# Mixture of experts on one core: TensorE's order fixed step by step, each pair's gates beside the preceding pair's down projection, and a group's gather in one piece

## The chip, the core and the metric

One core of a Trainium2 chip runs the whole program. Its engines each work through a queue of their own: TensorE (PE; its weight loads are listed apart as PEld), VectorE (DVE), ScalarE (ACT), GpSimd (POOL) and SyncE (SP), whose queue issues the transfers of weights. The metric is the device time of one execution in microseconds (us).

## The reference

An encoder of two layers on 256 tokens of width 1024. Layer 0 mixes tokens by multi-head latent attention, layer 1 by Hyena long convolutions. Each mixer is followed by a mixture of experts: 16 experts in four groups of four, of which a token takes the best group and in it the best two experts.

```
def hier_moe(h, wg, bg, we, be, w_gate, w_up, w_down):
    ...
    combine = jnp.sum(jax.nn.one_hot(expert, N_EXPERTS, dtype=jnp.float32) * weights[..., None], axis=1)
    combine = combine.astype(t.dtype)
    out = jnp.zeros_like(t)
    for e in range(N_EXPERTS):
        a = jax.nn.silu(t @ w_gate[e]) * (t @ w_up[e])
        out = out + combine[:, e:e + 1] * (a @ w_down[e])
    return out.reshape(B, S, D)
...
        x = x + g2[:, None, :] * hier_moe(h, moe_wg[i], moe_bg[i], moe_we[i], moe_be[i],
                                          moe_w_gate[i], moe_w_up[i], moe_w_down[i])
```

A gate and an up matrix are 1024 x 256 each, a down matrix 256 x 1024.

## The kernel before

The change lies in the function of the experts, `moe(l, ss)` (layer `l` is 0 or 1). Each expert has 64 slots for tokens. Tokens are brought into the slots, and results back to the tokens, by matmuls with one-hot matrices. Two experts are worked on at once, a pair, each in 64 columns of TensorE, so there are eight pairs, two to a group. The pieces, and the names that the trace has for them:

- `hot(g)`: VectorE makes the one-hots `OH` of group g (L1176). Those of the groups after the first wait for the last evacuation of the gather before (`evac`).
- `gather(g, h)`: half of the gathering matmuls of a group, 16 of 128x256 into two banks `xt_ps` (L1310). Each bank is emptied into `XT` in two halves, the first by ScalarE (L1317), the second by VectorE (L1319).
- `gate_up(pair)`: 16 matmuls into `gu_ps` (L1399; in the trace each f32 matmul is two records, so 32). Then, for the first pair of a group, `group_out`: four matmuls `oht_ps` (L1338) that turn the one-hots over, VectorE's copy to `OHT` (L1339) and the combining weights `ws` (L1343). Then ScalarE's silu `sg` (L1407) and VectorE's product `aa` (L1409), which takes `sg`, `ws` and `gu_ps`.
- `down(pair, aa)`: two transposes `at_ps` (L1417), VectorE's copy `aT` (L1419), eight matmuls `dn_ps` (L1426, 16 records), and for each of its two halves VectorE's `yg` (L1429), ScalarE's `yH` (L1431) and VectorE's rest `yL` (L1433).
- `scatter(pair, ys)`: eight matmuls `acc` (L1445) that add `yH` and `yL` to the four accumulators.

The loop over ten steps writes gate_up(step), after odd steps the gather of the next group, scatter(step - 2) and down(step - 1). That is the order in which the program is written, not the one in which it runs: a scheduler that simulates a timeline decides the order on every engine, and it also puts other work between: in layer 0 that of the Hyena filters (matmuls `fh`, `fn`, `fi`, `fg`, `ff`, with VectorE's work on `fab` and others) and `ada_ps` (L398), the conditioning of the next layer. Only for pair 0 is TensorE's order written out by hand, by `ordered()`. What stands inside keeps its order on TensorE, and each such block comes behind the end of the one before, the instruction in `tail[0]`:

```
    @contextmanager
    def ordered():
        with ExitStack() as z:
            if tail[0] is not None:
                z.enter_context(tc.issue_after(tail[0]))
            z.enter_context(tc.manual_schedule(engines={mybir.EngineType.PE}))
            yield
        tail[0] = next(i for i in reversed(nc.cur_bb.bb.instructions) if i.engine == mybir.EngineType.PE)
```

After step 0 stands a branch (`tc.If`, L1463) that all engines pass: behind it lies the case of an expert with more tokens than slots, which this input doesn't take. PSUM banks: two for `dn_ps`, `oht_ps`, `at_ps` and `xt_ps` together, one for `gu_ps`, four for `acc`. Weights come in pieces of 1 MB through a class `Stream`, which issues the next transfer when a piece has been used up (`st.done`). After the experts of layer 0 the accumulators are copied to `x` and squared (`scr`) for the next norm; after those of layer 1 they are copied (L1472) and sent out.

Of the kernel before, what the change touches and what calls it, by code (L numbers as in the profile page):

```python
# [11 lines left out]
F32 = mybir.dt.float32  # L12
# [7 lines left out]
P = 128  # L20
# [6 lines left out]
CAP = 64  # L27
# [143 lines left out]
def trunk(ctx, tc, A, out):  # L171
    nc = tc.nc
# [261 lines left out]
    tail = [None]  # L434
# [79 lines left out]
    q = psF("rb_ps")  # L514
# [647 lines left out]
    def moe(l, ss):  # L1162
        with ExitStack() as es:
# [134 lines left out]

            def gather(g, h):
                XTs, OH = prep[g]  # L1300
                XT = gp.tile([P, 4, 256], F32, name="XT", tag="XT", bufs=3 + l)
                XTs.append(XT)
                for k2 in (2 * h, 2 * h + 1):
                    q = psA("xt_ps")
                    for kk in range(2):
                        k = 2 * k2 + kk
                        i = 0
                        for src in (xH, xL):
                            for t in range(2):
                                nc.tensor.matmul(q[:, kk * 256:(kk + 1) * 256], src[:, t, k * P:(k + 1) * P], OH[:, t, :],  # L1310
                                                 start=(i == 0), stop=(i == 3))
                                i += 1
                    for kk in range(2):
                        k = 2 * k2 + kk
                        qv = q[:, kk * 256:(kk + 1) * 256]
                        if kk == 0:
                            eva = nc.scalar.activation(XT[:, k % 4, :], qv, AF.Identity, scale=a[:, k:k + 1], bias=b[:, k:k + 1])  # L1317
                        else:
                            evac[0] = nc.vector.tensor_scalar(XT[:, k % 4, :], qv, a[:, k:k + 1], b[:, k:k + 1], op0=ALU.mult, op1=ALU.add)  # L1319
                if g == 0 and h == 1:  # L1320

                    with tc.issue_after(eva.ins):
                        nc.scalar.activation(sm.tile([P, 1], F32, name="warm"), C("ones", 0, 1), AF.Silu)

            def group(g):
                hot(g)
                for h in range(2):
                    gather(g, h)


            def group_out(g, OH):
# [52 lines left out]
            with tc.tile_pool(name="moew", bufs=2) as wp:  # L1384
                def gate_up(pair):
                    g, p2 = divmod(pair, 2)
                    XT, OH = prep[g]
                    es2 = (2 * pair, 2 * pair + 1)
                    q = psG("gu_ps")
                    for h in range(2):  # L1390
                        if pair == 0:
                            with ordered():
                                gather(0, h)
                        GU = [st.get("gu", l, e, h).rearrange("p (k n) -> p k n", k=4) for e in es2]
                        with ordered() if pair == 0 else nullcontext():
                            for k in range(4 * h, 4 * h + 4):
                                for i in range(2):
                                    c0 = (2 * p2 + i) * CAP
                                    nc.tensor.matmul(q[i * 64:(i + 1) * 64, :], XT[h][:, k % 4, c0:c0 + CAP], GU[i][:, k % 4, :],  # L1399
                                                     start=(k == 0), stop=(k == 7))  # L1400
                        for e in es2:
                            st.done("gu", l, e, h)
                    if p2 == 0:
                        outs[g] = group_out(g, OH)
                    ws = outs[g][1]
                    sg = wp.tile([P, 256], F32, name="sg", tag="sg", bufs=l + 1)
                    nc.scalar.activation(sg, q[:, :256], AF.Silu)  # L1407
                    aa = wp.tile([P, 256], F32, name="aa", tag="aa", bufs=l + 1)
                    nc.vector.scalar_tensor_tensor(out=aa, in0=sg, scalar=ws[:, p2:p2 + 1], in1=q[:, 256:], op0=ALU.mult, op1=ALU.mult)  # L1409
                    return aa  # L1410

                def down(pair, aa):
                    g, p2 = divmod(pair, 2)
                    es2 = (2 * pair, 2 * pair + 1)
                    q = psA("at_ps")
                    for j in range(2):
                        nc.tensor.transpose(q[:, j * P:(j + 1) * P], aa[:, j * P:(j + 1) * P], ident)  # L1417
                    aT = wp.tile([P, 2, P], F32, name="aT", tag="aT", bufs=l + 1)
                    nc.vector.tensor_copy(aT, q[:, :256].rearrange("p (a b) -> p a b", a=2))  # L1419
                    DN = [st.get("dn", l, e).rearrange("p (k n) -> p k n", k=2) for e in es2]  # L1420
                    ys = []
                    for n in range(2):
                        q = psA("dn_ps")
                        for j in range(2):
                            for i in range(2):
                                nc.tensor.matmul(q[i * 64:(i + 1) * 64, :], aT[:, j, i * 64:(i + 1) * 64], DN[i][:, j, n * 512:(n + 1) * 512],  # L1426
                                                 start=(j == 0), stop=(j == 1))
                        yg = wp.tile([P, 512], F32, name="yg", tag="yg", bufs=l + 1)
                        nc.vector.tensor_tensor(yg, q, grow[1][:, n * 512:(n + 1) * 512], op=ALU.mult)  # L1429
                        yH = wp.tile([P, 512], F32R, name="yH", tag="yH")  # L1430
                        nc.scalar.copy(yH, yg)  # L1431
                        yL = wp.tile([P, 512], F32R, name="yL", tag="yL")
                        nc.vector.tensor_tensor(out=yL, in0=yg, in1=yH.bitcast(F32), op=ALU.subtract)  # L1433
                        ys.append((yH, yL))
                    for e in es2:
                        st.done("dn", l, e)
                    return ys

                def scatter(pair, ys):
                    g, p2 = divmod(pair, 2)  # L1440
# [8 lines left out]
                aas, yss, outs = {}, {}, {}  # L1449
                for step in range(10):  # L1450
                    if step == 7 and l == 0:
                        st.hold = 4
                    if step < 8:
                        aas[step] = gate_up(step)
                        if step % 2 == 1 and step < 7:
                            group(step // 2 + 1)
                    if 0 <= step - 2:
                        scatter(step - 2, yss.pop(step - 2))
                    if step == 0:

                        top = nc.values_load(most.bitcast(I32)[0:1, 0:1], min_val=0, max_val=2 ** 31 - 1)
                        fp = wp.tile([P, 512], F32, name="fb", tag="yg", bufs=l + 1)
                        with tc.If(top > int(np.float32(CAP).view(np.int32)), label=f"beyond{l}"):  # L1463
                            beyond(fp)
                    if 0 <= step - 1 < 8:
                        yss[step - 1] = down(step - 1, aas.pop(step - 1))
                ss = None if l else sm.tile([P, 2, 2], F32, name="ss", tag="ss")
                for t in range(2):
                    for n in range(2):
                        sl = slice(n * 512, (n + 1) * 512)  # L1470
                        if l:
                            (nc.scalar.copy if n else nc.vector.tensor_copy)(x[:, t, sl], acc[t, n])  # L1472
                            nc.sync.dma_start(out[:, t, sl], x[:, t, sl])
                        else:
                            scr = wp.tile([P, 512], F32, name="scr", tag="yg", bufs=1)
# [102 lines left out]
```

## Time and profile before

| | |
|---|---|
| device time, three runs | 675.87 us median, 675.6 to 677.37 |
| the profiled execution | 673.48 us, of which the profile's span is 671.7 |
| mean granted clock of TensorE | 0.968 of full speed |
| TensorE busy | 612.9 us, 91% of the span |
| VectorE, ScalarE busy | 387.3 us (58%), 235.1 us (35%) |
| DMA | 183.02 MB, mean 272 GB/s |

The profile was taken from one execution, whose time lies a little under the median of the three runs. All times in it count from the start of the span.

### The profile page before, as it was taken

Reading aid. Unit: us, or ns where it says so; the run is one execution under the profiler, and the core shown is the slowest. Engines: PE = TensorE matmul, PEld = TensorE weight load, DVE = VectorE, ACT = ScalarE, POOL = GpSimd, SP = SyncE. Lnnn points to the kernel's source line nnn. Section 1 sums busy time; section 2 is a strip of 40 time slices with the busy share of each in tenths; the row PEclk is TensorE's granted clock in tenths of the full one; section 3 lists DMA queues with packets and bytes.
Section 4 is the critical chain, followed back from the end, with each engine's and each line's share of the span. In section 5 each row is a group of like instructions: output and inputs, shape, how many; then the busy total and the mean of one; then the engine's idle time right before and its main releaser. Section 6 shows DMA issues by size and latency. Waiting matters only on the chain. (4 is left out here: it accounts for less than half of the span.)

```text
span 671.7 us, 8605 instructions
## 1 busy us (share of the span) xinstructions
PE 612.9 (91%) x3149; PEld 359.1 (53%) x3149; DVE 387.3 (58%) x894; ACT 235.1 (35%) x475; POOL 6.1 (1%) x61
## 2 busy tenths in 40 slices
PE   5988888999879789999997999999998899999996
PEld 2656444656655435335435979458766434444432
DVE  7648797895585453442476386478785723333333
ACT  4626553574244212201155644324413312111111
POOL 0000000000000000000000000000000000000000
PEclk9897979999988999999997999999999799999999
DMA  8963999452943789697996656880069278999701
GB/s 333 418 278 119 412 422 419 195 188 91 370 198 134 300 350 381 255 357 306 399 412 240 245 194 237 348 356 1 0 257 387 108 252 363 421 393 407 293 1 62
DMA packets 26818, 183.02 MB, mean 272 GB/s; under 512 B 3089, under 2 KB 3474, under 8 KB 5522
## 3 DMA queue, kind: packets, MB, share of 16 engines
q1 hardware_dynamic: 26192, 180.84, 68.1%
q10 hardware_dynamic: 578, 1.57, 0.6%
q8 instruction: 26, 0.43, 0.3%
q14 instruction: 22, 0.18, 0.1%
HBM read 181.35 MB, written 1.05 MB: 272 GB/s over the span
## 5 line engine op out<-in xcount | busy, mean ns | idle before, releaser
L1399 PE MATMUL gu_ps<-wt,XT 128*64 128x512 f32 x448 | 112.1, 599 | 8.1 <-DVE aa L1409 4.1
L1399 PEld LDWEIGHTS gu_ps<-wt,XT 128*64 128x64 f32 x448 | 33.8, 137 | 65.3 <-issue 54.7
L1429 DVE TENSOR_TENSOR yg<-dn_ps,g1row 128x512 f32<-128x512 f32 x32 | 22.0, 688 | 81.0 <-PE dn_ps L1426 80.0
L1426 PE MATMUL dn_ps<-wt,aT 128*64 128x512 f32 x224 | 57.5, 597 | 0.0
L1431 ACT CAST yH<-yg 128x512 fp32r<-128x512 f32 x32 | 19.8, 617 | 105.4 <-DVE yg L1429 105.4
L1068 PE MATMUL psu<-hT,wt 128*128 128x256 f32 x192 | 44.2, 381 | 0.0
L678 DVE TENSOR_TENSOR wt<-wt 128x512 fp32r<-128x512 f32 x66 | 41.8, 684 | 2.9 <-ACT wt L677 2.2
L1068 PEld LDWEIGHTS psu<-hT,wt 128*128 128x128 f32 x192 | 35.9, 191 | 9.4 <-issue 2.4
L677 ACT CAST wt<-wt 128x512 fp32r<-128x512 f32 x66 | 36.1, 619 | 13.7 <-PE psu L690 6.1
L1319 DVE TENSOR_SCALAR XT<-xt_ps,modA,modT 128x256 f32<-128x256 f32 x32 | 17.4, 543 | 40.4 <-ACT XT L1317 40.0
L398 PE MATMUL ada_ps<-wt,csil 128*32 128x512 f32 x264 | 38.7, 628 | 0.0
L1068 PE MATMUL psu<-zH,wt 128*128 128x256 f32 x192 | 38.3, 293 | 0.0
L1317 ACT ACTIVATE XT<-xt_ps,modT,modA 128x256 f32<-128x256 f32 x32 | 18.0, 564 | 50.1 <-PE xt_ps L1310 50.0
L1426 PEld LDWEIGHTS dn_ps<-wt,aT 128*64 128x64 f32 x224 | 17.3, 136 | 30.6 <-issue 29.1
L1068 PEld LDWEIGHTS psu<-zH,wt 128*128 128x128 f32 x192 | 30.3, 189 | 2.4 <-ACT up L1073 0.8
L1433 DVE TENSOR_TENSOR yL<-yg,yH 128x512 fp32r<-128x512 f32 x32 | 22.1, 690 | 14.5 <-ACT yH L1431 14.4
L1310 PE MATMUL xt_ps<-OH,xH 128*128 128x256 f32 x128 | 28.8, 307 | 0.7 <-DVE m L1268 0.6
L1310 PE MATMUL xt_ps<-OH,xL 128*128 128x256 f32 x128 | 27.4, 292 | 0.6 <-DVE xL L1262 0.5
L1310 PEld LDWEIGHTS xt_ps<-OH,xH 128*128 128x128 f32 x128 | 21.3, 197 | 11.4 <-issue 4.1
L1068 PE MATMUL psu<-zL,wt 128*128 128x256 f32 x96 | 27.0, 281 | 0.0
L1076 DVE SCALAR_TENSOR_TENSOR uc<-up,vec,uc 128x256 f32<-128x256 f32 x24 | 11.6, 483 | 26.1 <-ACT uc L1075 26.1
L690 PE MATMUL y_ps<-wt 128*128 128x512 f32 x96 | 24.6, 403 | 0.0
(357 smaller groups left out, 1094.1 us busy)
## 6 DMA issues: line engine op xcount, KB each, us to landing
wt<-in_gu SPq DMA_DIRECT2D x56, 1024.0 KB, 7.7
wt<-in_adas SPq DMA_DIRECT2D x40, 1024.0 KB, 10.5
wt<-in_dn SPq DMA_DIRECT2D x28, 1024.0 KB, 6.9
wt<-in_win SPq DMA_DIRECT2D x12, 1024.0 KB, 7.7
wt<-in_ada SPq DMA_DIRECT2D x8, 1024.0 KB, 17.7
wx<-in_gu SPq DMA_DIRECT2D x8, 1024.0 KB, 7.6
wt<-in_wo SPq DMA_DIRECT2D x4, 1024.0 KB, 5.7
wt<-in_wout SPq DMA_DIRECT2D x4, 1024.0 KB, 10.9
```

Of the source, the lines that this page charges most:

```text
L398: nc.tensor.matmul(q[g * 32:(g + 1) * 32, :], w.to_broadcast([P, 32]), W[:, g * 512:(g + 1) * 512], start=first, stop=(k == 7))
L677: nc.scalar.copy(Hi[:, sl], W[:, sl])
L678: nc.vector.tensor_tensor(Lo[:, sl], W[:, sl], Hi[:, sl].bitcast(F32), op=ALU.subtract)
L690: nc.tensor.matmul(yq[t, n], z[:, k, cols(t)], W[:, kk, n * 512:(n + 1) * 512], start=(k == 0 and f == 1), stop=(k == 7 and l == 1))
L1068: nc.tensor.matmul(q[:, :S], w[:, k, mm * P:(mm + 1) * P], h[:, k, :], start=(k == 0 and w is terms[0][0] and h is terms[0][1]), stop=(k = ...
L1310: nc.tensor.matmul(q[:, kk * 256:(kk + 1) * 256], src[:, t, k * P:(k + 1) * P], OH[:, t, :], start=(i == 0), stop=(i == 3))
L1317: eva = nc.scalar.activation(XT[:, k % 4, :], qv, AF.Identity, scale=a[:, k:k + 1], bias=b[:, k:k + 1])
L1399: nc.tensor.matmul(q[i * 64:(i + 1) * 64, :], XT[h][:, k % 4, c0:c0 + CAP], GU[i][:, k % 4, :], start=(k == 0), stop=(k == 7))
L1426: nc.tensor.matmul(q[i * 64:(i + 1) * 64, :], aT[:, j, i * 64:(i + 1) * 64], DN[i][:, j, n * 512:(n + 1) * 512], start=(j == 0), stop=(j = ...
L1429: nc.vector.tensor_tensor(yg, q, grow[1][:, n * 512:(n + 1) * 512], op=ALU.mult)
L1431: nc.scalar.copy(yH, yg)
L1433: nc.vector.tensor_tensor(out=yL, in0=yg, in1=yH.bitcast(F32), op=ALU.subtract)
```

## The change

Every step of the loop is now one block under `ordered()`: on TensorE gate_up(s), down(s - 1), scatter(s - 2), then what was the second half of gate_up and the first of down, as `gated(s)` (group_out in even steps, `sg`, `aa`, transposes, `aT`), and in odd steps the one-hots and both halves of the next group's gather. So `down` gets `aT` where it got `aa`. `tail[0]` is cleared before the loop and behind the branch. Numbers of buffers change: XT 2 in layer 0 and 4 in layer 1 (from 3 and 4), and sg, aa, yg, fb and scr the pool's two in both layers (from 1 in layer 0 and 2 in layer 1).

```diff
@@ -1298,7 +1298,7 @@
-                XT = gp.tile([P, 4, 256], F32, name="XT", tag="XT", bufs=3 + l)
+                XT = gp.tile([P, 4, 256], F32, name="XT", tag="XT", bufs=2 + 2 * l)
@@ -1321,11 +1321,6 @@
-            def group(g):
-                hot(g)
-                for h in range(2):
-                    gather(g, h)
@@ -1384,39 +1379,41 @@
                     for h in range(2):
                         if pair == 0:
-                            with ordered():
-                                gather(0, h)
+                            gather(0, h)
...
+                    return q
+
+
+                def gated(pair, q):
+                    g, p2 = divmod(pair, 2)
                     if p2 == 0:
-                        outs[g] = group_out(g, OH)
+                        outs[g] = group_out(g, prep[g][1])
                     ws = outs[g][1]
...
-                    return aa
-
-                def down(pair, aa):
-                    g, p2 = divmod(pair, 2)
-                    es2 = (2 * pair, 2 * pair + 1)
                     q = psA("at_ps")
                     for j in range(2):
                         nc.tensor.transpose(q[:, j * P:(j + 1) * P], aa[:, j * P:(j + 1) * P], ident)
                     aT = wp.tile([P, 2, P], F32, name="aT", tag="aT", bufs=l + 1)
                     nc.vector.tensor_copy(aT, q[:, :256].rearrange("p (a b) -> p a b", a=2))
+                    return aT
+
+                def down(pair, aT):
+                    es2 = (2 * pair, 2 * pair + 1)
@@ -1446,24 +1443,32 @@
                 for step in range(10):
                     if step == 7 and l == 0:
                         st.hold = 4
-                    if step < 8:
-                        aas[step] = gate_up(step)
+                    with ordered():
+                        q = gate_up(step) if step < 8 else None
+                        if 0 <= step - 1 < 8:
+                            yss[step - 1] = down(step - 1, aTs.pop(step - 1))
+                        if 0 <= step - 2:
+                            scatter(step - 2, yss.pop(step - 2))
+                        if step < 8:
+                            aTs[step] = gated(step, q)
                         if step % 2 == 1 and step < 7:
-                            group(step // 2 + 1)
-                    if 0 <= step - 2:
-                        scatter(step - 2, yss.pop(step - 2))
+                            g = step // 2 + 1
+                            hot(g)
+                            for h in range(2):
+                                gather(g, h)
                     if step == 0:
...
+                        tail[0] = None
-                    if 0 <= step - 1 < 8:
-                        yss[step - 1] = down(step - 1, aas.pop(step - 1))
```

What this moves, at three places, the first on two engines. In layer 1, on TensorE, from the down projection of pair 0 to the gather of group 2, before:

```order
L1426 MATMUL dn_ps<-wt,aT 64x512 x8
L1338 MATMUL oht_ps<-tok,OH 128x160 x2
L1445 MATMUL acc<-yH,OHT 128x512 x2
L1445 MATMUL acc<-yL,OHT 128x512 x2
L1338 MATMUL oht_ps<-tok,OH 128x160 x2
L1417 MATMUL at_ps<-cst,aa 128x128 x2
L1445 MATMUL acc<-yH,OHT 128x512 x2
L1399 MATMUL gu_ps<-wt,XT 64x512 x13
L1445 MATMUL acc<-yL,OHT 128x512 x2
L1426 MATMUL dn_ps<-wt,aT 64x512 x8
L1399 MATMUL gu_ps<-wt,XT 64x512 x3
L1310 MATMUL xt_ps<-OH,xH 128x256 x2
```

and after, the end of an even step and the step behind it (six of the eight acc ahead of oht left out):

```order
L1442 MATMUL acc<-yH,OHT 128x512
L1442 MATMUL acc<-yL,OHT 128x512
L1333 MATMUL oht_ps<-tok,OH 128x160 x4
L1410 MATMUL at_ps<-cst,aa 128x128 x2
L1392 MATMUL gu_ps<-wt,XT 64x512 x16
L1423 MATMUL dn_ps<-wt,aT 64x512 x8
```

The gates stand in one piece of 16, directly ahead of a down projection; scatter stands in one piece ahead of oht, where halves of it lay between oht and the transposes; and nothing lies between the transposes and oht.

On VectorE in the same even step, before:

```order
L1429 TENSOR_TENSOR yg<-dn_ps,g1row 128x512
L1433 TENSOR_TENSOR yL<-yg,yH 128x512
L1429 TENSOR_TENSOR yg<-dn_ps,g1row 128x512
L1339 CAST OHT<-oht_ps 128x256
L1343 TENSOR_REDUCE ws<-oht_ps 64x1 x2
L1339 CAST OHT<-oht_ps 128x256
L1343 TENSOR_REDUCE ws<-oht_ps 64x1 x2
L1409 SCALAR_TENSOR_TENSOR aa<-sg,ws,gu_ps 128x256
L1433 TENSOR_TENSOR yL<-yg,yH 128x512
L1419 COPY aT<-at_ps 128x256
```

and after:

```order
L1426 TENSOR_TENSOR yg<-dn_ps,g1row 128x512 x2
L1430 TENSOR_TENSOR yL<-yg,yH 128x512
L1334 CAST OHT<-oht_ps 128x256
L1338 TENSOR_REDUCE ws<-oht_ps 64x1 x2
L1334 CAST OHT<-oht_ps 128x256
L1430 TENSOR_TENSOR yL<-yg,yH 128x512
L1338 TENSOR_REDUCE ws<-oht_ps 64x1 x2
L1407 SCALAR_TENSOR_TENSOR aa<-sg,ws,gu_ps 128x256
L1412 COPY aT<-at_ps 128x256
```

The second yL has moved from behind aa to between the last OHT and ws.

On VectorE ahead of the branch in layer 0, before:

```order
L1409 SCALAR_TENSOR_TENSOR aa<-sg,ws,gu_ps 128x256
L1176 TENSOR_TENSOR OH<-cst,rk 128x256
L596 TENSOR_TENSOR fh<-fh_ps,fdec 128x512
L1461 TENSOR_LOAD most
L1463 COMPARE_AND_BRANCH
```

and after:

```order
L1176 TENSOR_TENSOR OH<-cst,rk 128x256
L1407 SCALAR_TENSOR_TENSOR aa<-sg,ws,gu_ps 128x256
L596 TENSOR_TENSOR fh<-fh_ps,fdec 128x512
L1412 COPY aT<-at_ps 128x256
L1467 TENSOR_LOAD most
L1469 COMPARE_AND_BRANCH
```

The copy aT of pair 0 has come ahead of the branch.

On TensorE at the end of layer 0's experts, before (the transposes are those of pair 7):

```order
L1417 MATMUL at_ps<-cst,aa 128x128 x2
L1445 MATMUL acc<-yH,OHT 128x512 x2
L1445 MATMUL acc<-yL,OHT 128x512 x2
L1426 MATMUL dn_ps<-wt,aT 64x512 x8
L398 MATMUL ada_ps<-wt,csil 32x512 x4
```

and after:

```order
L398 MATMUL ada_ps<-wt,csil 32x512 x4
L1410 MATMUL at_ps<-cst,aa 128x128 x2
L398 MATMUL ada_ps<-wt,csil 32x512 x4
L1423 MATMUL dn_ps<-wt,aT 64x512 x8
L1442 MATMUL acc<-yH,OHT 128x512
```

Two groups of ada now lie around these transposes, and two more among the last acc, where the old order has two, both behind this down projection; eight ada stand behind the experts in both.

## Rows read from the trace of the kernel before

**Rows 1.** The page's first part: busy time, share of span, instructions of TensorE and others
```profile
PE 612.9 (91%) x3149; PEld 359.1 (53%) x3149; DVE 387.3 (58%) x894; ACT 235.1 (35%) x475; POOL 6.1 (1%) x61
```

**Rows 2.** Windows: stretch of layer 0's experts, and one group of layer 1
```profile
core 0: us, PE busy (x) PEld busy (x) DVE busy (x) ACT busy (x) POOL busy (x), PEclk, DMA share, GB/s
220.36:324.38 104.02, 97.39 (x487) 48.49 (x487) 43.90 (x92) 19.37 (x37) 0.60 (x2) 1.00 0.84 326
...
573.15:605.73 32.58, 32.13 (x153) 14.12 (x153) 11.03 (x25) 5.39 (x10) 0.00 (x0) 1.00 0.99 405
```

**Rows 3.** Waits of TensorE in layer 0's experts: total, times, longest
```profile
engine line waited for: us in total, times, longest us
PE gu_ps L1399 <- DVE aa L1409: 3.7, 4, 1.3
PE fg_ps L625 <- DVE fab L621: 2.6, 2, 1.3
PE gu_ps L1399 <- DVEq L1463: 2.5, 1, 2.5
```

**Rows 4.** Waits of TensorE in layer 1's experts
```profile
PE acc L1445 <- DVE yL L1433: 0.8, 1, 0.8
PE gu_ps L1399 <- DVE aa L1409: 0.7, 3, 0.2
...
PE at_ps L1417 <- DVE ws L1343: 0.6, 3, 0.2
```

**Rows 5.** Timeline of TensorE in layer 1: start, duration, instruction, idle before
```profile
547.57 7.09 PE L1399 MATMUL gu_ps<-wt,XT 128*64 128x512 f32 x32 [1.37 <-DVEq L1463]
554.58 0.51 PE L1310 MATMUL xt_ps<-OH,xH 128*128 128x256 f32 x2
...
555.64 0.40 PE L1310 MATMUL xt_ps<-OH,xH 128*128 128x256 f32 x2
...
563.72 0.44 PE L1417 MATMUL at_ps<-cst,aa 128*128 128x128 f32 x2
564.09 2.79 PE L1399 MATMUL gu_ps<-wx,XT 128*64 128x512 f32 x12
566.72 3.60 PE L1426 MATMUL dn_ps<-wt,aT 128*64 128x512 f32 x16
570.25 0.46 PE L1338 MATMUL oht_ps<-tok,OH 128*128 128x160 f32 x2
570.54 0.67 PE L1445 MATMUL acc<-yH,OHT 128*128 128x512 f32 x2
571.04 0.62 PE L1445 MATMUL acc<-yL,OHT 128*128 128x512 f32 x2
```

**Rows 6.** Timeline of TensorE behind the experts of layer 0
```profile
350.83 1.92 PE L398 MATMUL ada_ps<-wt,csil 128*32 128x512 f32 x16
```

**Rows 7.** Timeline of the end of layer 1's experts
```profile
666.23 0.74 PE L1445 MATMUL acc<-yL,OHT 128*128 128x512 f32 x2 [0.79 <-DVE yL L1433]
666.77 1.07 ACT L1472 COPY x<-acc 128x512 f32<-128x512 f32 x2 [2.12 <-PE acc L1445]
```

**Rows 8.** Timeline of VectorE in an even step of layer 1
```profile
571.23 0.42 DVE L1339 CAST OHT<-oht_ps 128x256 fp32r<-128x256 f32 x1
...
572.61 0.48 DVE L1409 SCALAR_TENSOR_TENSOR aa<-sg,ws,gu_ps 128x256 f32<-128x256 f32 x1
573.01 0.69 DVE L1433 TENSOR_TENSOR yL<-yg,yH 128x512 fp32r<-128x512 f32 x1
```

**Rows 9.** Timeline of VectorE in a gather of layer 1
```profile
556.44 0.54 DVE L1319 TENSOR_SCALAR XT<-xt_ps,modA,modT 128x256 f32<-128x256 f32 x1 [0.85 <-ACT XT L1317]
```

**Rows 10.** Timeline of VectorE ahead of the branch, layer 0 and layer 1
```profile
219.51 0.69 DVE L596 TENSOR_TENSOR fh<-fh_ps,fdec 128x512 f32<-128x512 f32 x1
...
546.93 0.48 DVE L1409 SCALAR_TENSOR_TENSOR aa<-sg,ws,gu_ps 128x256 f32<-128x256 f32 x1
```

**Rows 11.** Windows at the branch of layer 0 and behind its experts, columns as in rows 2
```profile
217.85:222.00 4.15, 1.65 (x9) 0.74 (x10) 2.35 (x7) 1.51 (x3) 0.00 (x0) 1.00 0.99 349
352.75:356.44 3.69, 0.01 (x2) 0.01 (x1) 3.20 (x15) 0.85 (x3) 0.21 (x4) 0.86 1.02 422
356.44:362.00 5.56, 5.56 (x25) 3.57 (x25) 4.63 (x10) 5.56 (x13) 0.00 (x0) 0.50 0.31 84
```

More of the change, by code (lines that the diff above doesn't have):

```diff
@@ L1386, in gate_up @@
                     g, p2 = divmod(pair, 2)
-                    XT, OH = prep[g]
+                    XT = prep[g][0]
                     es2 = (2 * pair, 2 * pair + 1)
@@ L1391, in gate_up @@
                         if pair == 0:
-                            with ordered():
-                                gather(0, h)
+                            gather(0, h)
                         GU = [st.get("gu", l, e, h).rearrange("p (k n) -> p k n", k=4) for e in es2]
[L1395 to L1400, printed above, removed]
+                        for k in range(4 * h, 4 * h + 4):
+                            for i in range(2):
+                                c0 = (2 * p2 + i) * CAP
+                                nc.tensor.matmul(q[i * 64:(i + 1) * 64, :], XT[h][:, k % 4, c0:c0 + CAP], GU[i][:, k % 4, :],
+                                                 start=(k == 0), stop=(k == 7))
                         for e in es2:
                             st.done("gu", l, e, h)
+                    return q
+                def gated(pair, q):
+                    g, p2 = divmod(pair, 2)
                     if p2 == 0:
-                        outs[g] = group_out(g, OH)
+                        outs[g] = group_out(g, prep[g][1])
                     ws = outs[g][1]
-                    sg = wp.tile([P, 256], F32, name="sg", tag="sg", bufs=l + 1)
+                    sg = wp.tile([P, 256], F32, name="sg", tag="sg")
                     nc.scalar.activation(sg, q[:, :256], AF.Silu)
-                    aa = wp.tile([P, 256], F32, name="aa", tag="aa", bufs=l + 1)
+                    aa = wp.tile([P, 256], F32, name="aa", tag="aa")
                     nc.vector.scalar_tensor_tensor(out=aa, in0=sg, scalar=ws[:, p2:p2 + 1], in1=q[:, 256:], op0=ALU.mult, op1=ALU.mult)
-                    return aa
-                def down(pair, aa):
-                    g, p2 = divmod(pair, 2)
-                    es2 = (2 * pair, 2 * pair + 1)
                     q = psA("at_ps")
@@ L1427, in down @@
                                                  start=(j == 0), stop=(j == 1))
-                        yg = wp.tile([P, 512], F32, name="yg", tag="yg", bufs=l + 1)
+                        yg = wp.tile([P, 512], F32, name="yg", tag="yg")
                         nc.vector.tensor_tensor(yg, q, grow[1][:, n * 512:(n + 1) * 512], op=ALU.mult)
@@ L1448, in moe @@
                 tail[0] = None
-                aas, yss, outs = {}, {}, {}
+                aTs, yss, outs = {}, {}, {}
                 for step in range(10):
@@ L1452, in moe @@
                         st.hold = 4
-                    if step < 8:
-                        aas[step] = gate_up(step)
+                    with ordered():
[6 more added lines that the diff above has]
+                            aTs[step] = gated(step, q)
                         if step % 2 == 1 and step < 7:
-                            group(step // 2 + 1)
-                    if 0 <= step - 2:
-                        scatter(step - 2, yss.pop(step - 2))
+                            g = step // 2 + 1
+                            hot(g)
+                            for h in range(2):
+                                gather(g, h)
                     if step == 0:
                         top = nc.values_load(most.bitcast(I32)[0:1, 0:1], min_val=0, max_val=2 ** 31 - 1)
-                        fp = wp.tile([P, 512], F32, name="fb", tag="yg", bufs=l + 1)
+                        fp = wp.tile([P, 512], F32, name="fb", tag="yg")
                         with tc.If(top > int(np.float32(CAP).view(np.int32)), label=f"beyond{l}"):
                             beyond(fp)
-                    if 0 <= step - 1 < 8:
-                        yss[step - 1] = down(step - 1, aas.pop(step - 1))
+                        tail[0] = None
                 ss = None if l else sm.tile([P, 2, 2], F32, name="ss", tag="ss")
@@ L1474, in moe @@
                         else:
-                            scr = wp.tile([P, 512], F32, name="scr", tag="yg", bufs=1)
+                            scr = wp.tile([P, 512], F32, name="scr", tag="yg")
                             nc.scalar.activation(scr, acc[t, n], AF.Square, scale=1.0 / 32.0, accum_out=ss[:, n, t:t + 1])
```

## The prediction, made before the changed kernel was run

> **What bounds the kernel now.** I read the busy shares first: TensorE (PE) is busy 91% of the span [rows 1], so its queue, which runs in the order in which it stands, is where time is made or lost. Then the windows of the expert stages: one group of layer 1 (four experts, two pairs) takes 32.58 us, of which PE is busy 32.13, at a granted clock of 1.00; the long stretch of layer 0 takes 104.02 with PE busy 97.39 [rows 2]. So in layer 1 there is almost no idle time to take away, in layer 0 there are 6.6 us. Then the list of waits: in layer 0 PE waits 3.7 us for aa (the gated product, made by VectorE, DVE), 2.6 for fab (filter work), 2.5 at the branch [rows 3]; in layer 1 0.8 for yL, 0.7 for aa, 0.6 for ws [rows 4]. No row names a weight transfer as what PE waits for, though DMA is at a share of 0.99 in that group of layer 1; the new order takes the weights in the same sequence at about the same pace, so I cost the transfers at nothing, covered by the slots held ahead. If that cover went, a later load would stall the gates that use it.
>
> **The price of each block**, start to next start on PE, in layer 1 [rows 5]: 16 gate matmuls 547.57 to 554.58 = 7.01; one bank of the gather (8 matmuls of 128x256) 554.58 to 555.64 = 1.06, and after the first, with no change of shape, about 0.95, so 3.9 for four banks; two transposes 563.72 to 564.09 = 0.37; a down projection 566.72 to 570.25 = 3.53; half of oht 570.25 to 570.54 = 0.29; two acc matmuls 570.54 to 571.04 = 0.50, so 2.0 for eight. An ada group of eight records is about 1.0 (sixteen take 1.92), and these sixteen, at 350.83, are the first work behind the experts of layer 0 [rows 6]. (One matmul in the order is two records in the trace where it is f32.)
>
> **Layer 1 in the new order.** Without waits, from the gates of pair 1 to the last acc: 7 x 7.01 + 8 x 3.53 + 8 x 2.0 + 3 x 3.9 + 7 x 0.37 + 3 x 0.58 = 49.1 + 28.2 + 16.0 + 11.7 + 2.6 + 1.7 = 109.3 us. The old order needs 119.2 for this (547.57 to the end of the last pair of acc, 666.23 + 0.5, [rows 5, 7]): 2.1 of waits, and 7.8 of what the mixing itself costs (a gate block cut 13 + 3, and a change between 64-row and 128-row shapes at every cut; the second bank of the gather, with none, is cheaper than the first). That is what the change can win. Against it stand three new waits.
>
> First, the even step. gates(s), down(s-1) and scatter(s-2) end before oht starts, and only then DVE can make OHT, ws and aa, on which the transposes wait, and behind these, in PE's fixed queue, the next gates. Count from the end of down: acc to 2.0, oht to 2.6 (PE has nothing more). DVE has yg and a first yL (0.69 each, by yL's row) done by 1.5 and starts OHT at about 2.4. OHT, ws, OHT, ws take 571.23 to 572.61 = 1.38, the second yL now stands among them (0.6 of its 0.69), aa takes 0.48 [rows 8]: 2.4 + 1.38 + 0.6 + 0.5 = 4.9. PE waits 4.9 - 2.6 = 2.3, with the handover 2.4. Lower bound 1.75, if yL slips out of the chain; upper 3.0, if the first yL is late too, since ScalarE's yH stands between. Before, the gates of pair s+1 waited 0.7 for aa in three times [rows 4], because 13 of them, acc and a transpose lay over the chain. Three times: 7.2.
>
> Second, the gather. Its four banks now follow one another through two PSUM banks, and each bank is emptied by ScalarE and then by DVE, one after the other: DVE's part of the first bank starts at 556.44 and takes 0.54 [rows 9], so ends at 556.98, while PE, uninterrupted, would want the bank at about 556.6. With the handover 0.45 per gather; bounds 0 (the idle DVE starts sooner) and 1.0 (both banks late). Before, four gate records lay there. Three times: 1.35.
>
> Third, the branch after step 0. DVE now makes aT(0) before it. aa ends at 547.41 [rows 10], then two transposes and a copy (0.5 + 0.42) before DVE passes: gates(1) start at 548.5 instead of 547.57. In layer 0 fh hides part of the transposes, aT comes behind it: 221.05 instead of 220.36, +0.7.
>
> In the tail the last down waits for its aT, about 0.6, since only scatter lies before it. Sum for layer 1: 548.5 + 109.3 + 7.2 + 1.35 + 0.6 = 666.95 against 666.7 before: +0.25 on PE. The last two x copies, which now come one acc apart instead of together [rows 7], give back 0.45. Layer 1: **-0.2**.
>
> **Layer 0.** The same blocks, 109.3, and between them 50 records of filter matmuls at 0.13 (a 128x256 matmul, as one bank of the gather has it) = 6.5, and four ada groups in place of two: 4.0. Together 119.8. Waits: even steps 2 and 4 have two one-hots more in DVE's chain (+0.8) and some filter matmuls over it (-0.3): 2.9 each; step 6 2.4; gathers 1.35; the tail's aT lies under an ada group. 9.55. 221.05 + 119.8 + 9.55 = 350.4, against 350.83 before: **-0.4**. The two ada groups (2.0) no longer stand behind the experts. There PE is idle for 3.69 us anyway, until VectorE's norm is done [rows 11], so they gain only where they stood in PE's way; between 0 and 2.0 I take half: **-1.0**. The rest of the Hyena layer is scheduled anew in a like order: 0, with +-2.
>
> **Sum:** -0.2 - 0.4 - 1.0 = -1.6 us. On the profiled execution's 673.48 this is 671.9; the median of the runs shown is 675.87, 2.4 above it, and to that the forecast goes: **674.3 us**. In each layer some 10 us are won and as much is lost.
>
> **The rivals.**
> *The clock falls.* Rows: after a wait of 2.50 us at the branch the granted clock stayed 1.00 (window 217.85 to 222.00, PE busy 1.65 of 4.15); after 3.69 idle it was 0.50, that is 1.2 instead of 2.4 GHz, for 5.56 us [rows 11]. Work of 5.56 at 0.50 is 2.78 at full speed, so a fall costs 2.8. The change makes six waits of 2.4 to 2.9, each after 12 us of dense work, and a branch wait of 3.2 in layer 0, which lies between what held and what fell. If all seven fell: +19.5, 694; two make it slower than before by more than its measurement can tell, and that is the case on the other side: 674.3 + 5.6 = 679.9.
> The Trainium skill's "TensorE: Matmul & The Clock Gate", section "A second HAM failure mode: psum-queue depth-cycling", speaks against the change: a kernel that cycles through PSUM banks and idles briefly between groups of matmuls went back and forth between the two clocks, and lost the time there. By that rule each of the six even steps could pay, 674.3 + 16.8 = 691; by this trace's 2.50 us wait none does.
> *The fixed queue meets late filter work.* In layer 0 DVE also makes the filters, and PE waited 1.3 us twice for fab [rows 3]. In a fixed order a gather bank or an aT that stands behind such DVE work stops everything. Two fab waits that remain (2.6) and one more piece of 0.69 ahead of each of three gathers (2.1): 679.0.
> *More is won.* The even wait is at its lower bound (6 x 0.65 = 3.9) and the gather stalls at half: 1.35. For it: DVE is far from full. Against: yL's place in DVE's order is fixed. 669.0.
> That the change doesn't do what it says is excluded: the order on PE is as told, with a few filter matmuls between blocks.
>
> **How the numbers follow.** About 0.3% (2.0 us) is what a measurement can tell from no change. Chances: the sum as worked out, 672 to 676.5, 0.47; more won 0.19; late filter work 0.17; the clock, from two falls, 0.10; a Hyena layer that came out over 2 us differently 0.07. Faster (under 673.8): 0.4 of the first, the third case, part of the last: 0.41. Slower (over 677.9): clock, most of the late filter work: 0.25. Same: 0.34. The range leaves out most of the clock case and the edge of the gain: 668.8 to 680.0; the likeliest case alone has 672 to 676.5.
>
> **What would show it.** Gate blocks of 16 without a cut at 7.0; a wait of PE for aa in the list of waits (transposes for aa) of 1.75 to 3.0, six times; 0.3 to 0.6 at the gather, for the bank that DVE empties; gates(1) at +0.7 and +0.9 after the branch; the first ada group after the experts some 0.4 earlier. Wrong it would be if the clock in an even step is under 0.95, if PE waits for a weight load, or if the Hyena layer itself takes over 2 us more or less.

## The result, and the profile after

The changed kernel takes 679.61 us (median of nine runs, 677.88 to 680.78) against 675.87 before (nine runs): the ratio is 1.0053, 95% interval 1.0031 to 1.0074. It is 0.5% slower, by more than the measurement is uncertain; the forecast was a small gain. The number lies inside the forecast range, at its upper edge; the direction was wrong.

The profiled execution has a span of 678.4 us, 6.7 more than before, and a mean granted clock of 0.957 (0.968). The lower clock isn't that of one execution: in the nine runs of the changed kernel the mean is 0.957 to 0.962, in 58 runs of the kernel before, made beside the experiments, 0.960 to 0.973. TensorE's waits, with the same columns as in [rows 3, 4], first for the window from 195 to 360 us (experts of layer 0), then from 520 to 678 (layer 1):

```profile
PE at_ps L1410 <- DVE aa L1407: 7.0, 4, 2.4
...
PE xt_ps L1310 <- DVE XT L1319: 1.3, 3, 0.6
PE ada_ps L398 <- DMA wt<-in_adas: 1.2, 1, 1.2
PE gu_ps L1392 <- DVEq L1469: 0.7, 1, 0.7
```

```profile
PE at_ps L1410 <- DVE aa L1407: 9.1, 4, 2.4
PE gu_ps L1392 <- DVEq L1469: 1.2, 1, 1.2
...
PE xt_ps L1310 <- DVE XT L1319: 0.8, 3, 0.3
PE xt_ps L1310 <- DVE yg L1426: 0.7, 1, 0.7
```

The waits are those of the forecast: the transposes for aa, 2.4 at the longest. One even step of layer 1 on TensorE (start, duration, instruction):

```profile
577.72 0.57 PE L1333 MATMUL oht_ps<-tok,OH 128*128 128x160 f32 x4
580.73 0.41 PE L1410 MATMUL at_ps<-cst,aa 128*128 128x128 f32 x2 [2.43 <-DVE aa L1407]
581.06 8.79 PE L1392 MATMUL gu_ps<-wt,XT 128*64 128x512 f32 x32
589.68 1.89 PE L1423 MATMUL dn_ps<-wt,aT 128*64 128x512 f32 x8
```

and on VectorE:

```profile
578.11 0.42 DVE L1334 CAST OHT<-oht_ps 128x256 fp32r<-128x256 f32 x1
...
579.14 0.68 DVE L1430 TENSOR_TENSOR yL<-yg,yH 128x512 fp32r<-128x512 f32 x1
...
580.10 0.48 DVE L1407 SCALAR_TENSOR_TENSOR aa<-sg,ws,gu_ps 128x256 f32<-128x256 f32 x1
```

VectorE's chain is as it was worked out. What was not forecast is the third row on TensorE: the gates behind the wait take 581.06 to 589.68 = 8.62, where 7.01 stood in [rows 5]. Windows show why (columns as in [rows 2]; the clock is the third number from the right): an even step's wait, the first part of the gates behind it, and within it the first 1.00 us and a later stretch; then the gates of pair 2, which stand behind a gather and not behind a wait, the gates behind step 2 of layer 0, the first part of those behind the branch of layer 0, and a whole group of layer 1.

```profile
577.72:580.73 3.01, 0.58 (x6) 0.45 (x4) 2.77 (x9) 0.62 (x1) 0.00 (x0) 1.00 1.01 425
581.06:584.50 3.44, 3.44 (x13) 1.03 (x14) 0.42 (x1) 0.00 (x0) 0.00 (x0) 0.64 1.00 422
581.06:582.06 1.00, 1.00 (x7) 0.43 (x8) 0.42 (x1) 0.00 (x0) 0.00 (x0) 1.00 0.97 410
582.50:585.00 2.50, 2.50 (x8) 0.72 (x6) 0.00 (x0) 0.00 (x0) 0.00 (x0) 0.50 1.01 426
...
565.32:572.24 6.92, 6.92 (x33) 2.35 (x34) 1.52 (x4) 0.56 (x1) 0.00 (x0) 1.00 0.91 339
...
258.23:265.24 7.01, 7.01 (x31) 2.20 (x30) 1.65 (x4) 0.00 (x0) 0.00 (x0) 1.00 0.79 296
...
223.07:226.50 3.43, 3.43 (x10) 1.28 (x12) 1.38 (x3) 0.63 (x1) 0.00 (x0) 0.59 0.41 167
```

```profile
599.84:634.38 34.54, 31.83 (x154) 14.97 (x153) 11.23 (x25) 5.50 (x10) 0.00 (x0) 0.95 0.93 373
```

The granted clock is 1.00 during the wait and in the first 1.00 us of the gates, and then falls to 0.50, so that the first 3.44 us have 0.64. The same 16 matmuls of pair 2 run at 1.00 in 6.92. So a group takes 34.54 instead of 32.58 [rows 2], and the surplus, 1.96, is one fall (8.62 - 6.92 = 1.70) and little else. There are six such blocks: gates(1) behind both branches (8.59 and 8.58), pair 7 of layer 0 (330.48 to 338.58, 8.10) and pairs 3, 5 and 7 of layer 1 (8.62, 8.62, 8.61). Together they cost 9.6 us (and 0.26 in the transposes ahead of pair 7 of layer 0, which take 0.59 instead of 0.33). Only behind steps 2 and 4 of layer 0, where filter matmuls lie in the wait, the gates keep their clock.

Stage by stage, before and after, from the starts of the instructions named:

| stretch | before | after | difference |
|---|---|---|---|
| start to gates(1) of layer 0 | 220.36 | 223.07 | +2.7 |
| to the end of the last acc of layer 0 | 130.5 | 133.2 | +2.7 |
| to the first pse of the Hyena layer (norm) | 5.6 | 7.2 | +1.5 |
| to the last pst of the Hyena layer | 149.8 | 143.3 | -6.6 |
| to xT of layer 1's router | 11.9 | 11.8 | 0 |
| to gates(0) | 17.9 | 15.6 | -2.3 |
| to gates(1) | 11.6 | 13.4 | +1.8 |
| to the end of the last copy of x | 120.3 | 126.2 | +5.9 |
| to the end of the span | 3.9 | 4.7 | +0.8 |

Both layers of experts lost, and the Hyena layer between them won back more than half of it. The table is of two executions, 6.7 us apart; by the ratio of the nine runs the change costs 3.6. Two of its rows hold differences that the change didn't make: 1.4 of the first is there at the start of gates(0), ahead of all that the change moves, and the -2.3 is in code that it doesn't touch (see the last section).

The numbers of buffers changed together with the order, and no run takes them apart.

### The profile page after: what moved, and what is told of

It reads as the page before. It is cut to its first block, busy times and chain, and to the rows that moved or that the text cites. A ratio compares the mean times of both kernels' runs of the same rounds, so it can differ in the third digit from the quotient of the medians.

```text
span 678.4 us, 8617 instructions
## 1 busy us (share of the span) xinstructions
PE 610.0 (90%) x3149; PEld 361.7 (53%) x3149; DVE 389.4 (57%) x894; ACT 236.1 (35%) x475; POOL 6.1 (1%) x61
## 5 line engine op out<-in xcount | busy, mean ns | idle before, releaser
L1392 PE MATMUL gu_ps<-wt,XT 128*64 128x512 f32 x448 | 110.6, 637 | 1.9 <-DVEq L1469 1.9
L1423 PE MATMUL dn_ps<-wt,aT 128*64 128x512 f32 x224 | 52.3, 593 | 0.5 <-DVE aT L1412 0.5
L1405 ACT ACTIVATE sg<-gu_ps 128x256 f32<-128x256 f32 x16 | 6.1, 383 | 129.2 <-PE gu_ps L1392 127.6
L1407 DVE SCALAR_TENSOR_TENSOR aa<-sg,ws,gu_ps 128x256 f32<-128x256 f32 x16 | 7.7, 481 | 59.1 <-ACT sg L1405 58.8
L1442 PE MATMUL acc<-yH,OHT 128*128 128x512 f32 x64 | 26.8, 418 | 0.0
```

## The experiments

Theory A: the waits of 2.4 us in the even steps and the longer waits at the branches make TensorE's granted clock fall, and a fall costs the gates behind it 1.2 to 1.7 us, on top of the wait. The rivals are named with each run. Ratios are against runs of the kernel before on the same chip.

**1. Work in the wait.** Ten matmuls with weights of zero, added to an accumulator, fill the wait of the four even steps that were followed by slow gates.

```diff
+            zr = ep.tile([P, 1], F32R, name="zr")
+            nc.vector.tensor_scalar(zr, ident[:, 0:1], 0.0, None, op0=ALU.mult)
...
                         outs[g] = group_out(g, prep[g][1])
+                        if pair == 6 or pair and l:
+                            for i in range(10):
+                                nc.tensor.matmul(acc[i % 2, 0], zr.to_broadcast([P, P]), xH[:, 0, :512], start=False, stop=False)
```

> The changed kernel, with ten matmuls of 128x512 with weights of zero, added to an accumulator, behind oht in the even steps of pair 6 in layer 0 and pairs 2, 4 and 6 in layer 1: work for TensorE of 2.3 us in a wait of 2.4 us, which adds nothing to the result. The wait for aa stays as it is. Theory A (the wait makes the granted clock fall, and the gates behind it run at half speed for a part): these four gate blocks take 6.9 to 7.0 us instead of 8.6, 8.6, 8.6 and 8.1, so 3 x 1.7 + 1.2 = 6.3 us less than the changed kernel, 673.3. Rival B (the gates are slow for another reason, weights that come late or the DMA's traffic): the blocks stay at 8.6, the time at 679.6.

Measured: 674.87 us, ratio 1.0007 (0.9987 to 1.0027). The step on TensorE, and the first half of the gates as a window:

```profile
581.50 0.57 PE L1335 MATMUL oht_ps<-tok,OH 128*128 128x160 f32 x4
581.91 2.52 PE L1407 MATMUL acc<-xH,zr 128*128 128x512 f32 x10
584.51 0.41 PE L1415 MATMUL at_ps<-cst,aa 128*128 128x128 f32 x2
584.85 7.09 PE L1394 MATMUL gu_ps<-wt,XT 128*64 128x512 f32 x32
591.76 0.60 PE L1428 MATMUL dn_ps<-wt,aT 128*64 128x512 f32 x2
```

```profile
584.85:588.29 3.44, 3.44 (x17) 1.20 (x18) 0.42 (x1) 0.00 (x0) 0.00 (x0) 1.00 1.01 419
```

The transposes come as long after oht as before (3.0 us), nothing is taken from VectorE's chain, the DMA's share is 1.01, in the slow block 1.00, and the gates run at 1.00 in 6.91. All four blocks do (6.91 to 6.92). That is theory A, and rival B falls. The time gained only 0.46% of 675.87 = 3.1 us of the 6.3. In the profiled execution (678.84, the slowest of the twelve) layer 1 from gates(1) to the last copy gains 5.2 and layer 0 from gates(1) to the last acc 2.1, but stretches that the edit doesn't touch lose 2.8 (up to gates(1) of layer 0), 2.1 (layer 1's router, see the last section) and 1.0 (the Hyena layer). What kept the other eleven from gaining 6.3 is not shown.

**2. Half of it.** The same with five.

> As the run with ten zero matmuls, with five: 1.15 us of the wait of 2.4 are filled, 1.3 stay. In layer 0 a wait of 1.17, behind filter matmuls, was followed by gates at full clock. If that carries over, the four blocks of gates take 6.9 to 7.0, as with ten; if half the filling leaves half the fall, 7.7 to 7.9.

Measured: 675.90 us, ratio 1.0011 (0.9992 to 1.0029). All four blocks take 6.91 to 6.92. Half of the filling took away the whole fall, in all four; the profiled span, 672.6, is 5.8 shorter than the changed kernel's, the time by the two ratios 2.8. The idling that is left, on TensorE:

```profile
577.57 1.36 PE L1407 MATMUL acc<-xH,zr 128*128 128x512 f32 x5
580.17 0.41 PE L1415 MATMUL at_ps<-cst,aa 128*128 128x128 f32 x2 [1.24 <-DVE aa L1412]
```

**3. The wait taken away.** oht goes between the two halves of the same pair's gates.

```diff
                         for e in es2:
                             st.done("gu", l, e, h)
+                        if pair and p2 == 0 and h == 0:
+                            outs[g] = group_out(g, prep[g][1])
...
-                    if p2 == 0:
+                    if pair == 0:
                         outs[g] = group_out(g, prep[g][1])
```

> The changed kernel, with the four oht matmuls of pairs 2, 4 and 6 moved between the two halves of the same pair's gates, so that VectorE's OHT and ws lie under the second half. Theory A (an even step costs a wait of 2.4 us and a fall of the clock, 1.7 us in the gates behind it): three even steps of layer 1 at 4.1, step 6 of layer 0 at 3.6, steps 2 and 4 of layer 0 at 1.2 (part of their wait is under filter matmuls), less 1.2 for the shape changes: 679.6 - 17.1 = 662.5. Rival B (only the wait costs; what makes the gates slow is not tied to it): 3 x 2.4 + 2.4 + 2.4 - 1.2 = 10.8, 668.8. Rival C (the wait only moves, to sg or aT): 676 to 680.

Measured: 665.28 us, ratio 0.9866 (0.9832 to 0.9899), 12.6 us less than the changed kernel by the two ratios, between the numbers of A and B. In the stages it is more than A said: from gates(1) to gates(7) of layer 0 takes 98.7 instead of 107.4 (1.7 of it is gates(1), which kept the clock here behind the waits of the changed kernel, 2.20 and 0.67), layer 1 from gates(1) to the last copy 115.1 instead of 126.2, and the gates behind an even step take 6.92 at a clock of 1.00:

```profile
578.98:585.90 6.92, 6.92 (x34) 2.35 (x35) 1.13 (x3) 0.32 (x1) 0.00 (x0) 1.00 0.99 420
```

Rival C falls: there is no wait for aa in any even step. Most of what is missing went into the Hyena layer, whose 152.3 us (to the last pst) are 9.0 more than in the changed kernel: its order was made anew, with 96 records of ada in it as before, instead of 80, its entry runs at 0.50 behind an idle 3.8 us, and the clock falls once more within it (0.58 from 470.50 to 474.00). Layer 1's router takes 2.0 more.

**4 and 5. One layer at a time.** The changed loop in one layer, the former in the other.

> The changed loop in layer 1 alone; up to the branch of layer 1 the order is that of the kernel before on every engine. Theory A: all of layer 1's loss, three even steps with 1.7 us of slow gates and the branch with 1.7 and 1.0, shows: 6.5 us slower than the kernel before, 682.3. Rival D (the profiled executions mislead, the loss is layer 0's): within 1 us of 675.9.

> The changed loop in layer 0 alone; up to layer 1 the order is that of the changed kernel, the Hyena layer's included, behind it that of the kernel before. If the parts add up, what the changed kernel lost in all (3.7) less layer 1's 6.5: 2.8 us faster than the kernel before, 673.1; the experts of layer 0 themselves about 6 slower, the Hyena layer about 7 shorter. Rival D: 679 to 680.

Measured: layer 1 alone 682.97, ratio 1.0126 (1.0102 to 1.0150); layer 0 alone 672.21, ratio 0.9967 (0.9944 to 0.9989). Alone in layer 1 the change loses 8.5 us (rival D falls), alone in layer 0 it gains 2.2. The profiled execution of the second doesn't put this gain into layer 0 and the Hyena layer: up to the last pst it is 0.6 longer than the kernel before, and it gains 2.3 in layer 1's router, which the edit doesn't touch. The four slow blocks of layer 1 stand in the trace of the first as in the changed kernel (8.59, 8.61, 8.62, 8.61). The two ratios add up to 1.0093 where the changed kernel has 1.0053; the intervals just allow it.

**6. The branch.** The transposes and aT of pair 0 go behind the branch (`turned` holds the lines of `gated` from `at_ps` on).

```diff
+                        if step == 1:
+                            aTs[0] = turned(aTs[0])
                         if 0 <= step - 1 < 8:
                             yss[step - 1] = down(step - 1, aTs.pop(step - 1))
...
                             aTs[step] = gated(step, q)
+                            if step:
+                                aTs[step] = turned(aTs[step])
```

> The changed kernel, with the two transposes and aT of pair 0 put behind the branch of step 0, between the gates of pair 1 and the down projection of pair 0, in both layers. Theory A (the longer wait at the branch makes the clock fall): the wait is shorter by 1.0 to 1.9 us in each layer, and the gates of pair 1 run in 7.0 to 7.5 us instead of 8.6: 1.9 + 1.6 + 1.0 + 1.6 = 6.1 us less than the changed kernel, about 673.5. Rival E (the wait at the branch hangs on the branch itself, not on aT): within 1 us of 679.6, the gates of pair 1 at 8.6.

Measured: 677.53 us, ratio 1.0038 (1.0012 to 1.0065). In the profile the gates of pair 1 take 7.02 in both layers, and oht to gates(1) is shorter by 1.3 in layer 0 (4.02 for 5.32) and 1.6 in layer 1 (2.52 for 4.11). Rival E falls: it was aT. That the shorter wait kept the clock is not shown for layer 0: TensorE idles 2.81 us there ahead of gates(1), in the changed kernel 2.19 and 0.67. And the sum was too large by what comes back: the down projection of pair 0 now waits behind the transposes for its aT, 0.95 us in each layer (552.97 to 553.93 in layer 1), and the step 6 of layer 0 fell further (8.61 for 8.10). The profiled span is 2.7 us shorter than that of the changed kernel, the ratios give 1.0, with intervals of 1.8 and 1.5 to either side; so of the 6.1 at most some 3 are seen, and the gain in time is not clear of noise.

**7. The gather.** Not in one piece: in steps 3 and 5 each bank is followed by two of the eight matmuls of scatter.

```diff
                             evac[0] = nc.vector.tensor_scalar(XT[:, k % 4, :], qv, a[:, k:k + 1], b[:, k:k + 1], op0=ALU.mult, op1=ALU.add)
+                    if between:
+                        between(k2)
...
+                            ys = yss.pop(step - 2) if woven else None
                             for h in range(2):
-                                gather(g, h)
+                                gather(g, h, (lambda part: scatter(step - 2, ys, part)) if woven else None)
```

> The changed kernel, with the gather not in one piece: in steps 3 and 5 each of its four banks is followed by two of the eight acc matmuls of the scatter. Theory A says of the gather that PE waits there for a bank to be emptied, 0.6 us in each: the waits for XT go, 4 x 0.6 = 2.4 us less, 677.2, the rest as in the changed kernel, its slow gates too. Rival F (the gather in one piece is the main loss): 4 us or more less, 675 or below.

Measured: 680.90 us, ratio 1.0069 (1.0045 to 1.0094), as the changed kernel. Both theories were too hopeful. The waits for XT of steps 3 and 5 are gone, but the first bank now waits for a bank that yg of the down projection still holds:

```profile
594.09 0.44 PE L1412 MATMUL at_ps<-cst,aa 128*128 128x128 f32 x2
594.98 0.50 PE L1310 MATMUL xt_ps<-OH,xH 128*128 128x256 f32 x2 [0.45 <-DVE yg L1428]
```

From the end of the down projection to the next gates it is 594.09 to 600.83 = 6.74, in the changed kernel 593.21 to 599.84 = 6.63. The gather in one piece costs nothing that this way of breaking it up would give back.

**8. oht between the gates, and aT behind the branch.**

> Both edits, oht between the halves of the gates and aT of pair 0 behind the branch. What cover gave is 13 us against the changed kernel; with the 6.1 of the branch, if the two are apart as theory A has it: 660.5. If what is won in layer 0 is lost again in front of the Hyena layer, where the wait for the norm stands, 663.

Measured: 659.41 us, ratio 0.9766 (0.9739 to 0.9793): 2.3% faster than the kernel before, 2.9% faster than the changed one. A group of layer 1 takes 30.54, with neither wait nor fall:

```profile
555.53:586.07 30.54, 30.26 (x153) 14.47 (x153) 11.25 (x25) 5.50 (x10) 0.00 (x0) 1.00 1.00 409
```

The DMA's share is 1.00 there too. That the time lies near the 660.5 is in part luck: of the 10.0 us between the profiled spans of run 3 and this one, 5.1 lie in the Hyena layer, which the edit of the branch doesn't touch. With the gather woven as well:

> All three edits: the former with the gather woven into the scatter in steps 3 and 5. 2.4 us less than without: 658.

Measured: 661.11 us, ratio 0.9770 (0.9741 to 0.9799): no gain over the former, as in run 7.

**9. All waits kept, all falls meant to go.** Ten zero matmuls as in run 1, and aT behind the branch.

> Both the ten zero matmuls in the four even steps and aT of pair 0 behind the branch: the waits for aa of 2.4 us stay, all six falls of the clock go. If the clock is what made the change slower than before, the blocks of gates are 6.9 to 7.0 throughout, except none; 679.6 less 6.3 less 6.1, between 667 and 671 (the lower end if the router of layer 1 keeps its clock), and so clearly faster than the kernel before. If the slow gates only move to other stretches, 675 or above.

Measured: 672.02 us, ratio 0.9947 (0.9929 to 0.9966), 1.1% less than the changed kernel by the two ratios and faster than the kernel before, though the transposes of the even steps still come 3.0 us after oht. In the profile five of the six blocks run in 6.9 to 7.0. gates(1) of layer 0 fell (8.56), behind the same wait behind which they kept the clock in run 6. The 672 is a little above the 667 to 671 expected. That the order without its falls gains in the experts is not shown: in the profiled execution (675.52, the slowest of the six) layer 1 from gates(1) to the last copy takes 120.4 us, 120.3 in the kernel before, and layer 0 from gates(1) to the last acc 131.5, 130.5 before, with one fall of 1.6 in it. So the experts are about level without falls (and with aT behind the branch), near the -0.2 and -0.4 of the forecast; what is gained lies in the Hyena layer, 5.0, less 1.5 ahead of it.

## Why the prediction was wrong

**The step that failed** is in the rivals: "*by this trace's 2.50 us wait none does*", that is, that a wait of 2.4 in the even steps would leave the clock where a wait of 2.50 at the branch had left it, and a chance of 0.10 for the clock. The waits came to 2.43, as forecast, and behind every one of them that had no work in it TensorE fell below full speed: all 16 in the profiles of the changed kernel and runs 4 to 7. One wait of one execution was taken for a bound. At that branch TensorE idles 2.50 to 2.93 us ahead of gates(1) of layer 0 (in one piece, or in two around the transposes) in all twelve kernels profiled; the gates kept the clock in six and lost it in six, and the kernel before was one that kept it. Runs 1, 2 and 9 show that it is the idling: in all 12 even steps with work in the same wait the gates stay at 1.00. The rule of the Trainium skill that the prediction weighed ("TensorE: Matmul & The Clock Gate", section "A second HAM failure mode: psum-queue depth-cycling") describes what happened: brief idling between groups of matmuls, and a clock that goes to and fro. The idling here is for aa, not for a PSUM bank, and filling it cured the fall.

**The size of a fall** was taken at 2.8 from [rows 11]; it measured 1.2 to 1.7 (8.10 to 8.62 for 6.92), in runs 1, 3 and 7 up to 2.5 (9.42 and 9.44). With six falls the rival's own mechanism gives 674.3 + 9.6 = 683.9. That the time stayed inside the range, and came within 0.3 of the rival's 679.9 for two falls of 2.8, is luck: six came, and the Hyena layer gave back what no term had. All three signs named for being wrong came: the clock (0.80 over the gates behind a wait), a wait for weights (2.6 us for ada behind the experts of layer 0), and the Hyena layer.

**Block by block, layer 1:** gates without a cut 6.92 (7.01 forecast), the even step's wait 2.43 (2.4), the last down's wait for aT 0.5 (0.6): right. The group without its fall would be 34.54 - 1.70 = 32.84, and the forecast's blocks sum up to 33.2 (7.01 x 2 + 3.53 x 2 + 2.0 x 2 + 3.9 + 0.37 x 2 + 0.58 + 2.4 + 0.45). "More is won" wanted waits of 1.75 and didn't come. The gather waits 0.8 for XT in its three groups and 0.7 for a bank of yg, 1.5 where 1.35 stood. The last copies end 1.27 behind the start of the last two acc, 1.61 before, 0.3 of the 0.45 forecast; but from there to the end of the span it is 0.8 more, for which no term stood: the four transfers of the result start at 672.65 to 674.58, before from 665.01 on. So layer 1's +8.5 (gates(0) to the end of the span) is the -0.2 forecast, 6.7 for four falls, 0.9 at the branch and 0.8 at the end; 0.3 is left.

**The branch** was mis-sized in both layers: gates(0) to gates(1) is +1.3 in layer 0 (16.99 for 15.69) where +0.7 stood, and +1.8 in layer 1 where +0.9 stood. In layer 0, on TensorE and VectorE:

```profile
217.75 0.68 PE L1333 MATMUL oht_ps<-tok,OH 128*128 128x160 f32 x4
...
220.92 0.68 DVE L596 TENSOR_TENSOR fh<-fh_ps,fdec 128x512 f32<-128x512 f32 x1
221.15 0.41 PE L1410 MATMUL at_ps<-cst,aa 128*128 128x128 f32 x2 [2.19 <-DVE aa L1407]
221.60 0.43 DVE L1412 COPY aT<-at_ps 128x256 f32<-128x256 f32 x1
...
223.07 1.45 PE L1392 MATMUL gu_ps<-wt,XT 128*64 128x512 f32 x4 [0.67 <-DVEq L1469]
```

Two things had no term. All four oht now stand behind the gates of pair 0, where two lay between their halves, so VectorE's OHT and ws for both are in the chain ahead of aa: from the last oht to aa it is 2.78 instead of 1.89. And the gates don't start when aT ends, at 222.03, but 1.04 later (0.74 in layer 1), where they came 0.16 behind fh [rows 10] and, in layer 1, behind aa. In run 6, without aT ahead of the branch, it is 0.16 again in both layers; why aT costs more than its copy stays open. The one-hot that moved ahead of aa costs nothing here: it was ahead of the branch before, too.

**Layer 0's end** was forecast at 350.4 and came at 356.3. Of the 5.9, 2.0 are the start of gates(1) (1.4 of it is there at the start of gates(0), ahead of all that the change moves), 1.67 and 1.18 the two falls; 1.0 is left. It is a difference of two terms: from gates(1) to the last acc TensorE waits 7.2 us where 9.55 stood, since steps 2 and 4 wait 0.32 and 1.17, not 2.9, with filter matmuls in the wait; and the work is longer, down projections 30.1 for 28.2 and gathers 12.9 for 11.7, as other matmuls stand between their parts. The rival of late filter work isn't it: of two waits of 1.3 for fab only the one ahead of the branch is left, and 0.6 for fgs is new.

**The Hyena layer** was mis-sized the other way: -6.6 where -1.0 stood, and without it the 3.6 by the ratio would be some 10. From rows: 16 fewer records of ada, 2.0; the waits inside, 1.3 instead of 2.8; and its entry. Before, TensorE idles 3.69 ahead of pse and then runs 5.56 us at 0.50 [rows 11]. After, ada that waits for its weights lies there, and the entry runs at 0.68 for 5.57 us, 1.0 us less lost:

```profile
357.69 1.06 PE L398 MATMUL ada_ps<-wt,csil 128*32 128x512 f32 x8 [1.25 <-DMA wt<-in_adas]
360.14 1.93 PE L398 MATMUL ada_ps<-wt,csil 128*32 128x512 f32 x8 [1.39 <-DMA wt<-in_adas]
363.43 0.47 PE L1025 MATMUL pse<-cst,hx 128*128 128x128 f32 x1 [1.35 <-DVE hx L495]
```

That is 4.5 of 6.6; the rest is the scheduler's new order and stays open. Part of the gain is paid ahead of it: pse comes 7.2 instead of 5.6 after the last acc. That layer 0 and the Hyena layer together gain isn't shown: in the profile of run 5 they come to +0.6, from the start of the span on.

## What to carry to other kernels

A fixed order that puts a short chain of another engine alone between two dense stretches of TensorE can cost twice: the wait, and a lower clock behind it. So lay the instruction that starts the chain (here oht) where TensorE has work for as long as the chain takes, and if that can't be, half a wait's worth of work in it was enough here to keep the clock. A wait that kept the clock in one profile is no bound, neither for a wait elsewhere nor for the same one in the next kernel: price a new wait with and without a fall, at the difference that a block of the kernel shows between the two speeds.

## What was not expected of the hardware

The length of a wait doesn't decide alone whether the clock falls. In run 6 gates(1) of layer 0 kept it behind an idle 2.81 us, in run 9 they lost it behind an idle 2.84, with the same instructions ahead; the even steps lost it behind 2.43 in the changed kernel and in runs 4 to 7. The first rows are of run 6, the second of run 9 (timeline, and the window of the gates' first 3.2 us):

```profile
221.81 1.08 PE L1392 MATMUL gu_ps<-wt,XT 128*64 128x512 f32 x4 [2.81 <-DVEq L1476]
```

```profile
221.81:225.00 3.19, 3.19 (x16) 1.40 (x18) 0.43 (x1) 0.57 (x1) 0.00 (x0) 1.00 0.86 336
```

```profile
223.79 1.12 PE L1394 MATMUL gu_ps<-wt,XT 128*64 128x512 f32 x2 [2.84 <-DVEq L1481]
```

```profile
223.79:227.00 3.21, 3.21 (x8) 1.09 (x10) 0.42 (x1) 0.57 (x1) 0.00 (x0) 0.51 0.88 342
```

And run 3, whose edit doesn't touch this branch and which has the waits of the changed kernel there (2.20 and 0.67), kept the clock. The first 3.43 us of its gates:

```profile
223.47:226.90 3.43, 3.43 (x16) 1.41 (x18) 1.38 (x3) 0.63 (x1) 0.00 (x0) 1.00 0.46 186
```

The router of layer 1 shows the same with code that the change doesn't touch. In the kernel before it ran at 0.81, in the changed one at 1.00, with waits of the same length (the first two 0.45 and 1.14, and 0.46 and 1.14):

```profile
518.13:536.00 17.87, 13.92 (x80) 8.64 (x80) 13.29 (x44) 7.21 (x16) 0.00 (x0) 0.81 0.39 154
```

```profile
518.55:534.14 15.59, 11.27 (x80) 6.84 (x80) 13.21 (x44) 7.21 (x16) 0.00 (x0) 1.00 0.37 138
```

That is 2.3 us without a change in the code, and what decides it stays open. A difference of half a per cent in this kernel can hold such a stretch, and is better read from its stages than from its total.
